# Feature-major products in two matmuls per block of 128 instead of three, and one adaLN vector computed a stage later

## The chip, the cores and the metric

The kernel runs on one core of a Trainium2 chip, as one program on five engines: TensorE (PE in the rows, with PEld for its loads of weights), VectorE (DVE), ScalarE (ACT), GpSimd (POOL) and SyncE (SP), which here only issues DMAs. The metric is the device time of one execution in microseconds (us); lower is better.

## The reference

Two transformer blocks run on 256 tokens of width 2048, all in float32. Cut to what the change touches:

```
def first_block(x, ...):
    z = rms_norm(x, pre_mix_g) @ w_in            # q, k, v, u
    ...                                           # chunked attention, multi-scale pool, w_o
    h = rms_norm(x, pre_ffn_g)
    up = causal_dwconv(h @ w_up, conv_w, conv_b)  # 3 taps over tokens
    y = (gelu(up[..., :5632]) * up[..., 5632:]) @ w_down
    return x + rms_norm(y, post_ffn_g)

def second_block(x, c, ctx, c_ctx, ...):
    shift1, scale1, gate1, shift2, scale2, gate2 = split(silu(c) @ w_ada + b_ada, 6)
    # the context gets its own shift1, scale1 from c_ctx
    hc = modulate(rms_norm(ctx, norm1_g), cshift1, cscale1)
    ...                                           # keys and values of ctx and x, attention, w_br, w_out
    h = modulate(rms_norm(x, norm2_g), shift2, scale2)
    return x + gate2 * ((silu(h @ w_ff_gate) * (h @ w_ff_up)) @ w_ff_down)
```

## The kernel before

**Products.** Each float32 operand is held as two parts, a high part h rounded to the matmul's format and the rest l, and each product is made of three matmuls, ah·bh + ah·bl + al·bh (`mm3`, L334 to L336). There are two ways to lay a product out. *Token-major* (`token_major`): 128 tokens of activations are the stationary operand, 512 columns of weights stream past them, three matmuls of 512 columns. *Feature-major* (`feature_major`): 128 columns of weights are stationary and all 256 tokens stream, so that the result has features on partitions; per block kb of 128 inputs that is three matmuls of 256 columns (weight h with activation h, weight h with activation l, weight l with activation h), and 16 blocks make one product of 48 matmuls in one PSUM bank. The kernel makes 192 feature-major products: 8 for u and 16 for q and k in block 1, 84 in the first feed-forward (42 blocks of 128 features, two halves each), 84 in the second; 192 x 16 = 3072 triplets.

**Weights.** `Stream` sends all weights in the order of use as pieces of 128x1024 through four buffers w (DMAs on SP, L203). `prep` makes their parts: ScalarE casts h (L236), VectorE subtracts l (L237), into rings of five buffers. A piece holds eight slabs of 128x128 groups; `done` is called after each slab of 512 columns, frees a buffer after every second, and emits the next `prep`.

**adaLN.** The vectors silu(c) @ w_ada + b_ada are made on VectorE: one step (L516) multiplies a 128x512 piece of w_ada with a row of silu(c) held on all partitions and sums. There are 512 steps over 384 pieces v (four buffers, DMAs on SP, L210); the first 128 pieces give shift1 and scale1 for c and for the context (two steps each), then come sh2, gate1, sc2 and gate2 with 64 pieces each. `done` emits `pace` steps per slab, by `PACE` (stage; feature-major, token-major), up to `limit` pieces; `S.finish()` emits what is left at the end of a stage.

**Side work.** Everything beside the stream of products is written as generators in `Side`; each tick (one per slab, roughly) advances at most `per` of them, and `side.drain()` ticks until all have ended, with no product emitted between. The order in which instructions are emitted is the order on each engine.

**Stages.** Block 1 (v, then q and k, then u, the other half of v, q and k, out projection), its feed-forward `ffn1` (six groups of up to eight blocks: the group's feature-major products with `act` on each, then four token-major chunks of 512 columns that add the group's part of w_down to y), then block 2: keys and values of context and x (`token_major` with four token tiles, six chunks), attention, w_br and w_out, and `ffn` again for the second feed-forward.

**The context.** During `ffn1`, `ctx_norm` normalises the context: for each of two token tiles it loads four chunks of 512 columns (L843), sums their squares, takes the factor (`rstd`, L403 to L406, the power on GpSimd), loads the chunks again (L850) and for each multiplies by the factor (L852), transposes on TensorE (L429), scales and shifts (L436 on ScalarE or L438 on VectorE, four each) and splits in h and l (L329, L330). Its loads go through two buffers. Its first act is

```
        while len(self.ada_done) < 8:
            yield 1
```

so that it starts only when the first 128 pieces of w_ada are through; it is queued at the first chunk of the third group (`gi == 2`). At the last chunk of the fifth of the six groups stands

```
            if gi == len(GROUPS) - 2 and c == 3 and t == 1:
                side.drain()
                S.finish()
                side.drain()
```

Of the kernel before, what the change touches and what calls it, by code (L numbers as in the profile page):

```python
# [33 lines left out]
PACE = ((0.6, 0.6), (0.5, 0.6), (0.0, 0.9), (0.05, 0.6), (0.2, 0.25))  # L35
# [234 lines left out]
class Kernel:  # L270
# [33 lines left out]

    def slot(self, i, dt):
        return self.spool.tile([P, 4096], dt, name=f"slot{i}", tag=f"slot{i}")
# [32 lines left out]
    def feature_major(self, xh, xl):  # L339

        bank = self.ob()
        self.S.pace = self.pace[0]
        for s in range(4):
# [232 lines left out]
    def block1(self):  # L576
# [4 lines left out]
        hh, hl = (self.slot(i, F32R).rearrange("p (k t) -> p k t", k=KB) for i in (0, 1))  # L581
# [25 lines left out]
        self.ada_begin({0: 0, 1: 4}, 192)  # L607

        ah, al = (self.slot(i, F32R).rearrange("p (k t) -> p k t", k=KB) for i in (2, 3))
# [10 lines left out]
        inv = self.g(64)  # L620
        nc.gpsimd.dma_start(tab, a["rb"])
# [35 lines left out]
        def uproj():  # L657
            for fb in range(8):
                bank = self.feature_major(hh, hl)
                nc.scalar.copy(ut[:, fb, 16:], bank[:, :256])  # L660
                if fb % 2:
                    side.add(pool(fb // 2))

        def qkproj(which):
            for j in range(4):
                bank = self.feature_major(hh, hl)
                self.split(qk[:, 2 * which, j, :], qk[:, 2 * which + 1, j, :], bank[:, :256])
# [126 lines left out]
    def out_proj(self, ah, al, state):  # L794
# [3 lines left out]
        hh, hl = (self.slot(i, F32R).rearrange("p (k t) -> p k t", k=KB) for i in (0, 1))  # L798
# [4 lines left out]
        st = {}  # L803
# [27 lines left out]
        self.ffn1(hh, hl, st["x"], lambda: self.norm_t(st["xs"], 1, hh, hl))  # L831
# [25 lines left out]
    def ffn(self, hh, hl, first, act, chunk_end, mid, tail=0):  # L857

        self.products, self.side.limit, self.side.per = 0, 5, 2
        banks = self.token_major([(hh, hl, 0), (hh, hl, 1)], self.staged(mid))  # L860
        pr = self.slot(self.prslot, F32R).rearrange("p (s k t) -> p s k t", s=2, k=8)
        first(banks, pr)
        total = 0
        for gi, grp in enumerate(GROUPS):
            last = gi == len(GROUPS) - 1
            total += len(grp)
            for n, i in enumerate(grp):
                if i > 1:
                    act(i, 0, self.feature_major(hh, hl), pr, n)
                    act(i, 1, self.feature_major(hh, hl), pr, n)  # L870
# [15 lines left out]
    def ffn1(self, hh, hl, x, mid):  # L886
        nc, a, side = self.nc, self.a, self.side
        S = self.S
# [4 lines left out]
        ch, cl = (self.slot(i, F32R).rearrange("p (k t) -> p k t", k=KB) for i in (2, 3))  # L893
# [3 lines left out]

        def act(i, half, bank, pr, n):
            f = half * NFB + i
            z = tmp[half]()  # L900
            w0, w1, w2, b = (self.vec(n, f, 1) for n in ("conv_w0", "conv_w1", "conv_w2", "conv_b"))
            nc.scalar.activation(z, bank[:, :256], AF.Identity, scale=w2, bias=b)  # L902
            nc.vector.scalar_tensor_tensor(z[:, 1:], bank[:, :255], w1, z[:, 1:], op0=ALU.mult, op1=ALU.add)  # L903
            nc.vector.scalar_tensor_tensor(z[:, 2:], bank[:, :254], w0, z[:, 2:], op0=ALU.mult, op1=ALU.add)
            if half == 0:
                za[n % 2] = z
                side.add(gelu(z))
                return

            def emit(a=za[n % 2]):  # L910
                p = pbuf()
                nc.vector.tensor_mul(p, a, z)
                return p
            side.add(self.product(pr, n, emit))

        za = {}

        def gelu(z):
            yield 1
            nc.scalar.activation(z, z, AF.Gelu_apprx_tanh)  # L920
            yield 1
# [5 lines left out]
        def chunk_end(gi, c, t, bank):  # L927
# [11 lines left out]
            if gi == len(GROUPS) - 2 and c == 3 and t == 1:  # L939
# [3 lines left out]
                assert S.vdone == 192 and len(self.ada_done) == 12  # L943
# [75 lines left out]
        h2, l2 = (self.slot(i, F32R).rearrange("p (k t) -> p k t", k=KB) for i in (0, 1))  # L1019
# [15 lines left out]
        self.ffn(hh, hl, first, act, chunk_end, mid, tail=4)  # L1035
# [31 lines left out]
    def block2(self):  # L1067
# [87 lines left out]
        oah, oal = (self.slot(i, F32R).rearrange("p (k t) -> p k t", k=16) for i in (2, 3))  # L1155
# [224 lines left out]
        mh, ml = (self.slot(i, F32R).rearrange("p (k t) -> p k t", k=KB) for i in (0, 1))  # L1380
# [34 lines left out]
        hh, hl = (self.slot(i, F32R).rearrange("p (k t) -> p k t", k=KB) for i in (2, 3))  # L1415
# [35 lines left out]
        sg, pb = self.ring(256, 2), self.ring(256, 2)  # L1451
        outr = a["out"].rearrange("(t p) d -> p t d", p=P)

        def act(i, half, bank, pr, n):
            if half == 0:
                za[n % 2] = z = sg()
                nc.scalar.activation(z, bank[:, :256], AF.Silu)
                return
            z = pb()
            nc.vector.tensor_mul(z, bank[:, :256], za[n % 2])  # L1460
            side.add(self.product(pr, n, lambda: z))

# [38 lines left out]
        self.ffn(hh, hl, first, act, chunk_end, lambda: self.norm_t(last["xs"], 1, hh, hl, self.g2, self.ada_v["sh2"]), tail=4)  # L1501
# [23 lines left out]
```

## Time and profile before

| | |
|---|---|
| time, median of three runs | 2772.29 us (2771.5 to 2775.25) |
| the profiled execution: its own time | 2772.85 us |
| its span, first to last instruction | 2771.1 us |
| PE busy | 2721.5 us, 98% of the span |
| DVE, ACT, POOL busy | 72%, 46%, 6% |
| the chain that ended last | PE 83%, DVE 3%, ACT 2% |

The span is what the trace covers; 1.75 us lie outside it. A matmul's duration in the rows is longer than the time to the next one, since matmuls overlap: how fast they follow each other is read from their starts.

### The profile page before, as it was taken

To read this page: it belongs to the slowest core of one execution; us is meant where nothing else is said; L and a number is where in the kernel's file an instruction comes from. 1 tells how busy PE (TensorE), PEld (TensorE's weight loads), DVE (VectorE), ACT (ScalarE), POOL (GpSimd) and SP (SyncE) were. 2 spreads that over 40 slices of the span, in tenths; PEclk is the share of its full clock that TensorE was granted. 3 is DMA by queue.
4 is the path that set the end of the run, shared out by engine and by line. 5 is a ranking of instruction groups with operands and counts; after the bars stand their busy time and mean duration, and the time that the engine had idled before them with its cause. 6 is when DMAs were issued, how large, how long until landed. Compare 5 with 4: busy or idle time off the path is not lost.

```text
span 2771.1 us, 43473 instructions
## 1 busy us (share of the span) xinstructions
PE 2721.5 (98%) x16726; PEld 2435.5 (88%) x16726; DVE 1986.2 (72%) x3258; ACT 1287.1 (46%) x1810; POOL 159.0 (6%) x215
## 2 busy tenths in 40 slices
PE   7999999999999999999999999999999999999999
PEld 6988798989898988788877888888889999898988
DVE  4888787888889856756477877678675565655465
ACT  4444455545455545422366665534354434343433
POOL 1010000000000000211011110100000000000000
PEclk9999999999999999999999999999999999999999
DMA  7667677676789854656555544599667676755565
GB/s 247 211 232 247 219 230 253 229 251 229 242 280 320 283 189 161 214 184 231 200 175 182 168 163 141 176 332 323 232 199 233 222 231 222 231 191 190 184 200 164
DMA packets 195696, 610.39 MB, mean 220 GB/s; under 512 B 22736, under 2 KB 22928, under 8 KB 194464
## 3 DMA queue, kind: packets, MB, share of 16 engines
q1 hardware_dynamic: 183024, 562.12, 60.5%
q0 software_dynamic: 12320, 45.25, 5.1%
q8 instruction: 131, 2.15, 0.3%
q14 instruction: 77, 0.63, 0.1%
q10 hardware_dynamic: 144, 0.25, 0.0%
HBM read 592.81 MB, written 14.71 MB: 219 GB/s over the span
## 4 chain that ended last, share of the span: by engine, by line
PE 83%; DVE 3%; ACT 2%; issue 1%; POOL 0%; ACTq 0%; DVEq 0%
PE bank L334 27%; PE bank L335 27%; PE bank L336 27%; DVE l L237 1%; PE bank L1227 1%; ACT h L236 1%; ACT G L454 0%; ACT slot L329 0%; PE bank L429 0%; ACT G L436 0%; PE bank L1201 0%; DVE slot L935 0%; PE bank L1216 0%; DVE slot L962 0%; DVE G L438 0%
## 5 line engine op out<-in xcount | busy, mean ns | idle before, releaser
L237 DVE TENSOR_TENSOR l<-w,h 128x1024 fp32r<-128x1024 f32 x870 | 1063.6, 1226 | 536.3 <-ACT h L236 526.0
L236 ACT CAST h<-w 128x1024 fp32r<-128x1024 f32 x870 | 907.8, 1049 | 842.4 <-PE bank L336 418.6
L334 PE MATMUL bank<-slot,h 128*128 128x256 f32 x3088 | 876.2, 284 | 4.4 <-DVE slot L330 4.1
L336 PE MATMUL bank<-slot,l 128*128 128x256 f32 x3088 | 875.1, 283 | 0.9 <-DVE l L237 0.9
L335 PE MATMUL bank<-slot,h 128*128 128x256 f32 x3088 | 874.9, 283 | 0.0
L334 PE MATMUL bank<-h,slot 128*128 128x512 f32 x2112 | 835.2, 395 | 9.1 <-ACT slot L329 4.3
L335 PE MATMUL bank<-l,slot 128*128 128x512 f32 x2112 | 826.7, 391 | 8.1 <-DVE l L237 8.1
L336 PE MATMUL bank<-h,slot 128*128 128x512 f32 x2112 | 826.2, 391 | 0.1
L334 PEld LDWEIGHTS bank<-slot,h 128*128 128x128 f32 x3088 | 593.9, 192 | 5.3 <-issue 4.3
L336 PEld LDWEIGHTS bank<-slot,l 128*128 128x128 f32 x3088 | 593.8, 192 | 1.2 <-DVE l L237 1.2
L335 PEld LDWEIGHTS bank<-slot,h 128*128 128x128 f32 x3088 | 593.9, 192 | 0.5
L334 PEld LDWEIGHTS bank<-h,slot 128*128 128x128 f32 x2112 | 398.4, 189 | 97.9 <-issue 7.4
L335 PEld LDWEIGHTS bank<-l,slot 128*128 128x128 f32 x2112 | 398.5, 189 | 90.2 <-DVE l L237 11.9
L336 PEld LDWEIGHTS bank<-h,slot 128*128 128x128 f32 x2112 | 398.1, 188 | 85.7 <-DVE slot L330 1.7
L516 DVE CUSTOM_DVE_ANT_0 G<-v,G 128x512 bf16<-128x512 f32 x512 | 386.7, 755 | 10.7 <-DMA v<-wada 8.5
L329 ACT CAST slot<-bank 128x512 fp32r<-128x512 f32 (+1 forms) x141 | 71.0, 528 | 131.0 <-PE bank L336 64.3
L330 DVE TENSOR_TENSOR slot<-bank,slot 128x512 fp32r<-128x512 f32 (+1 forms) x141 | 82.7, 610 | 44.4 <-ACT slot L329 44.2
L902 ACT ACTIVATE G<-bank,G 128x256 f32<-128x256 f32 x88 | 49.7, 565 | 115.5 <-PE bank L336 111.3
L903 DVE SCALAR_TENSOR_TENSOR G<-bank,G 128x255 f32<-128x255 f32 x88 | 42.4, 482 | 44.5 <-ACT G L902 44.5
L329 ACT CAST slot<-G 128x256 fp32r<-128x256 f32 (+1 forms) x114 | 52.0, 457 | 42.7 <-DVE G L438 23.9
L1244 ACT ACTIVATE G<-bank,G 128x512 f32<-128x512 f32 x64 | 49.8, 780 | 45.1 <-DVE G L1238 44.9
L330 DVE TENSOR_TENSOR slot<-G,slot 128x256 fp32r<-128x256 f32 (+1 forms) x114 | 55.3, 485 | 14.3 <-ACT slot L329 13.9
(198 smaller groups left out, 1307.6 us busy)
## 6 DMA issues: line engine op xcount, KB each, us to landing
v<-wada SPq DMA_DIRECT2D x384, 256.0 KB, 4.1
w<-wup SPq DMA_DIRECT2D x176, 512.0 KB, 4.3
w<-wgu SPq DMA_DIRECT2D x176, 512.0 KB, 3.4
w<-wdn SPq DMA_DIRECT2D x88, 512.0 KB, 4.1
w<-wfd SPq DMA_DIRECT2D x88, 512.0 KB, 3.3
w<-w SPq DMA_DIRECT2D x66, 512.0 KB, 4.6
w<-w2g SPq DMA_DIRECT2D x64, 512.0 KB, 3.3
w<-w2kv SPq DMA_DIRECT2D x52, 512.0 KB, 3.8
```

What stands on the lines that cost most here:

```text
L236: self.nc.scalar.copy(h, w)
L237: self.nc.vector.tensor_sub(l, w, h.bitcast(F32))
L329: self.nc.scalar.copy(h, src)
L330: self.nc.vector.tensor_sub(l, src, h.bitcast(F32))
L334: t.matmul(out, ah, bh, start=start, stop=False)
L335: t.matmul(out, ah, bl, start=False, stop=False)
L336: t.matmul(out, al, bh, start=False, stop=stop)
L516: nc.vector.tensor_tensor_reduce(out=self.junkv.bitcast(mybir.dt.bfloat16), in0=w, in1=self.adat[:, slot * 512:(slot + 1) * 512], scale=1. ...
L902: nc.scalar.activation(z, bank[:, :256], AF.Identity, scale=w2, bias=b)
L903: nc.vector.scalar_tensor_tensor(z[:, 1:], bank[:, :255], w1, z[:, 1:], op0=ALU.mult, op1=ALU.add)
L1227: nc.tensor.transpose(bank[:, k * P:(k + 1) * P], src[:, k * P:(k + 1) * P], self.ident)
L1244: nc.scalar.activation(d, bank, AF.Exp, bias=mx, scale=rq, accum_out=s)
```

## The change

Activations that feed feature-major products now lie in one tile of 128x8192 (`pair`) as [h of block kb, l of block kb], so that one matmul of 512 columns makes weight h with both parts; the second matmul of 256 columns adds weight l with h to the left half. The two halves of the bank are added when the bank is emptied (`folded`: a copy of the right half on ScalarE, an addition of the left half to it on VectorE), and convolution, SiLU, q and k splits then read the folded result from SBUF, mostly one product later. The vector sh2 (64 pieces of w_ada) is no longer made by the end of `ffn1` but in block 2's key and value stage, and three paces are changed.

```
-PACE = ((0.6, 0.6), (0.5, 0.6), (0.0, 0.9), (0.05, 0.6), (0.2, 0.25))
+PACE = ((0.5, 0.6), (0.27, 0.62), (0.0, 1.7), (0.05, 0.6), (0.2, 0.25))
...
+    def pair(self, i):
+        t = self.spool.tile([P, 8192], F32R, name=f"pair{i}", tag=f"pair{i}")
+        x = t.rearrange("p (k n) -> p k n", k=KB)
+        return x, x[:, :, :256], x[:, :, 256:]
...
-    def feature_major(self, xh, xl):
+    def feature_major(self, x):
...
-                self.mm3(bank[:, :256], h[:, j * P:(j + 1) * P], l[:, j * P:(j + 1) * P],
-                         xh[:, kb, :], xl[:, kb, :], kb == 0, kb == KB - 1)
+                hj, lj = h[:, j * P:(j + 1) * P], l[:, j * P:(j + 1) * P]
+                if kb < KB - 1:
+                    t.matmul(bank, hj, x[:, kb, :], start=kb == 0, stop=False)
+                    t.matmul(bank[:, :256], lj, x[:, kb, :256], start=False, stop=False)
+                else:
+                    t.matmul(bank[:, :256], lj, x[:, kb, :256], start=False, stop=False)
+                    t.matmul(bank, hj, x[:, kb, :], start=False, stop=True)
...
+    def folded(self, bank, out):
+        z = self.half()
+        self.nc.scalar.copy(z, bank[:, 256:])
+        self.nc.vector.tensor_add(out, bank[:, :256], z)
+        return out
...
-        if kind == 0:
-            self.ada_begin({k: k for k in range(4)}, self.S.limit)
...
-        self.ada_begin({0: 0, 1: 4}, 192)
+        self.ada_begin({0: 0, 1: 4}, 128)
...
-                bank = self.feature_major(hh, hl)
-                nc.scalar.copy(ut[:, fb, 16:], bank[:, :256])
+                self.folded(self.feature_major(hx), ut[:, fb, 16:])
...
         def act(i, half, bank, pr, n):
+            last = i == NFB - 1 or i % 8 == 7
+            if i > 1:
+                side.until(lambda: half not in busy)
+                busy.add(half)
+                bank = self.folded(bank, xq[half])
+            gen = acted(i, half, bank[:, :256], pr, n, int(i > 1 and not last))
+            if last or i < 2:
+                next(gen)
+            side.add(gen)
...
-                assert S.vdone == 192 and len(self.ada_done) == 12
+                assert S.vdone == 128 and len(self.ada_done) == 8
```

**TensorE, a feature-major product of `ffn1`.** The tile numbers after the names are buffers; bank is PSUM, slot and pair hold the activations, h and l the parts of the weights; the last column is the output. Before:

```order
L334 MATMUL bank_71<-slot_2138,h_82 128x256
L335 MATMUL bank_71<-slot_2139,h_82 128x256
L336 MATMUL bank_71<-slot_2138,l_87 128x256
L334 MATMUL bank_71<-slot_2138,h_82 128x256
L335 MATMUL bank_71<-slot_2139,h_82 128x256
L336 MATMUL bank_71<-slot_2138,l_87 128x256
```

and of the change:

```order
L358 MATMUL bank_73<-pair_1775,h_85 128x512
L359 MATMUL bank_73<-pair_1775,l_90 128x256
L358 MATMUL bank_73<-pair_1775,h_85 128x512
L359 MATMUL bank_73<-pair_1775,l_90 128x256
```

Two instructions stand for three, and the columns are the same, 768 per block.

**TensorE, the context's transposes.** Before, the transposes of a context chunk (L429) stand alone among products; this is the second of the eight:

```order
L429 MATMUL bank_74<-G 128x128 x4
L334 MATMUL bank_72<-slot_2138,h_86 128x256
L335 MATMUL bank_72<-slot_2139,h_86 128x256
L336 MATMUL bank_72<-slot_2138,l_91 128x256
```

In the change (L450 is the same line) the first of the eight stands among the products of the fifth group's third and fourth chunk; the other seven stand in one piece, at the fifth group's last chunk (L342 to L344 are its token-major matmuls), ahead of the first feature-major product of the sixth group:

```order
L342 MATMUL bank_72<-h_84,slot_2671 128x512
L343 MATMUL bank_72<-l_89,slot_2671 128x512
L344 MATMUL bank_72<-h_84,slot_2671 128x512
L450 MATMUL bank_74<-G 128x128 x4
L450 MATMUL bank_75<-G 128x128 x4
L450 MATMUL bank_76<-G 128x128 x4
L450 MATMUL bank_77<-G 128x128 x4
L450 MATMUL bank_74<-G 128x128 x4
L450 MATMUL bank_75<-G 128x128 x4
L450 MATMUL bank_76<-G 128x128 x4
L358 MATMUL bank_73<-pair_1775,h_85 128x512
```

**VectorE at the same place of the change.** L981 adds the last chunk to y, L879 multiplies a context chunk by its factor, L459 scales and shifts four blocks, L338 is the low part of a split, L424 and L426 are `rstd`, L238 is the low part of a piece of weights.

```order
L981 TENSOR_TENSOR slot_2515<-bank_72,slot_2515 128x512
L338 TENSOR_TENSOR pair_2516<-G,pair_2516 128x4x128
L879 TENSOR_SCALAR G<-G 128x512
L459 TENSOR_SCALAR G<-bank_75,G 128x128 x4
L338 TENSOR_TENSOR pair_2516<-G,pair_2516 128x4x128
L879 TENSOR_SCALAR G<-G 128x512
L338 TENSOR_TENSOR pair_2516<-G,pair_2516 128x4x128
L424 TENSOR_REDUCE G<-G 128x1
L426 TENSOR_SCALAR G<-G 128x1
...
L879 TENSOR_SCALAR G<-G 128x512
L338 TENSOR_TENSOR pair_2516<-G,pair_2516 128x4x128
L238 TENSOR_TENSOR l_89<-w_80,h_84 128x1024
```

Before, VectorE has pieces of weights, `act` and adaLN steps between one context chunk's operations and the next one's; here it has none of them between the last addition to y and the next piece of weights.

## Rows read from the trace of the kernel before

**Rows 1.** The page: busy time, share of the span and instructions of the engines.
```profile
PE 2721.5 (98%) x16726; PEld 2435.5 (88%) x16726; DVE 1986.2 (72%) x3258; ACT 1287.1 (46%) x1810; POOL 159.0 (6%) x215
```

**Rows 2.** The page, costliest groups: line, engine, operation, output<-inputs, sizes, count | busy us, mean ns | idle just before and who ended most of it. The first two are one of the three feature-major lines and one of the three token-major lines.
```profile
L334 PE MATMUL bank<-slot,h 128*128 128x256 f32 x3088 | 876.2, 284 | 4.4 <-DVE slot L330 4.1
L334 PE MATMUL bank<-h,slot 128*128 128x512 f32 x2112 | 835.2, 395 | 9.1 <-ACT slot L329 4.3
L516 DVE CUSTOM_DVE_ANT_0 G<-v,G 128x512 bf16<-128x512 f32 x512 | 386.7, 755 | 10.7 <-DMA v<-wada 8.5
```

**Rows 3.** Timeline of TensorE, start us, duration us, where a feature-major product of `ffn1` ends and a token-major chunk begins. Between the first row shown and the second lie 32 matmuls of 256 columns, between the last two lie 31 of 512.
```profile
699.74 0.28 PE L336 MATMUL bank<-slot,l 128*128 128x256 f32 x1
...
703.70 0.28 PE L336 MATMUL bank<-slot,l 128*128 128x256 f32 x1
703.82 0.40 PE L334 MATMUL bank<-h,slot 128*128 128x512 f32 x1
704.05 0.40 PE L335 MATMUL bank<-l,slot 128*128 128x512 f32 x1
...
704.52 0.40 PE L334 MATMUL bank<-h,slot 128*128 128x512 f32 x1
...
711.78 0.39 PE L336 MATMUL bank<-h,slot 128*128 128x512 f32 x1
```

**Rows 4.** Busy time by stretches: from:to, length, then busy us of each engine (instructions), granted clock of PE, share of DMA, GB/s. In turn: u in block 1; a stretch of `ffn1` with feature-major products alone; the fifth group's feature-major part, with context work; one chunk of keys in block 2's key and value stage.
```profile
112.00:157.00 45.00, 42.24 (x320) 40.40 (x319) 40.08 (x79) 20.33 (x39) 12.24 (x8) 0.96 0.55 175
500.00:550.00 50.00, 50.00 (x419) 50.00 (x418) 44.05 (x79) 25.86 (x35) 0.00 (x0) 1.00 0.65 225
890.00:925.00 35.00, 35.00 (x295) 35.00 (x295) 33.39 (x64) 19.36 (x30) 0.54 (x1) 1.00 0.85 290
1234.00:1278.00 44.00, 43.90 (x194) 36.05 (x193) 30.62 (x59) 10.81 (x13) 8.99 (x9) 1.00 0.59 207
```

**Rows 5.** Groups by line and shape, columns as in rows 2: operations of 256 columns that read a PSUM bank.
```profile
L660 ACT COPY G<-bank 128x256 f32<-128x256 f32 x8 | 3.0, 380 | 0.0
L902 ACT ACTIVATE G<-bank,G 128x256 f32<-128x256 f32 x88 | 49.7, 565 | 115.5 <-PE bank L336 111.3 <-DVE G L904 2.6 <-PE bank L1030 1.6
L1460 DVE TENSOR_TENSOR G<-bank,G 128x256 f32<-128x256 f32 x42 | 17.9, 425 | 24.4 <-PE bank L336 24.3
```

**Rows 6.** Timelines of single engines, context work in `ffn1`: start, duration, engine, line. The two GpSimd rows are the power in `rstd` and the second loads; then VectorE's multiplication of a chunk by the factor and its part of `rstd`, and the sum of a chunk's squares on ScalarE.
```profile
789.05 1.52 POOL L406 TENSOR_TENSOR G<-G 128x1 f32<-128x1 f32 x1 [10.38 <-DVE G L405]
790.54 1.11 POOL L850 DMA_DIRECT2D G<-ctx  x2
811.46 0.48 DVE L852 TENSOR_SCALAR G<-G 128x512 f32<-128x512 f32 x1
788.63 0.15 DVE L403 TENSOR_REDUCE G<-G 128x1 f32<-128x4 f32 x1
788.81 0.15 DVE L405 TENSOR_SCALAR G<-G 128x1 f32<-128x1 f32 x1
777.13 0.63 ACT L454 ACTIVATE G<-G 128x512 f32<-128x512 f32 x1
777.66 0.19 ACT L454 ACTIVATION_READ_ACCUMULATOR G<-G 128x1 f32 x1
```

**Rows 7.** The chain that ended last, start, duration, what: the same kinds of operations one behind the other (a chunk's multiplication, its four scalings, cast and subtraction), where x is normalised after `ffn1`.
```profile
1112.99 0.72 ACT G L973
1114.26 1.42 ACT G L436 x4
1115.70 0.63 ACT slot L329
1116.35 0.69 DVE slot L330
```

**Rows 8.** Time from issue to landing of the context's loads (256 KB each), first and second ones; then of w_ada's pieces, and of the key and value spills, in the key and value stage.
```profile
DMA to landing us min/median/max: 3.3/5.4/7.4
DMA to landing us min/median/max: 3.6/6.2/7.5
v<-wada SPq DMA_DIRECT2D x64, 256.0 KB, 3.7
kv<-slot POOLq DMA_DIRECT2D x24, 256.0 KB, 3.0
```

**Rows 9.** Timeline of TensorE: the transposes of the context's last chunk, between two matmuls of 256 columns.
```profile
897.13 0.28 PE L336 MATMUL bank<-slot,l 128*128 128x256 f32 x1
897.25 0.60 PE L429 MATMUL bank<-G 128*128 128x128 f32 x4
897.60 0.36 PE L334 MATMUL bank<-slot,h 128*128 128x256 f32 x1
897.80 0.28 PE L335 MATMUL bank<-slot,h 128*128 128x256 f32 x1
```

**Rows 10.** Busy time by stretches, as rows 4, around the norm ahead of `ffn1`, where TensorE waits for VectorE and ScalarE.
```profile
330.00:335.00 5.00, 2.43 (x10) 1.23 (x8) 4.30 (x8) 1.67 (x5) 0.55 (x1) 1.00 0.28 105
335.00:340.00 5.00, 3.51 (x10) 2.32 (x11) 4.86 (x7) 4.40 (x10) 0.00 (x0) 0.66 0.44 125
340.00:345.00 5.00, 5.00 (x24) 4.03 (x23) 4.30 (x9) 1.00 (x3) 0.55 (x1) 0.66 0.58 189
345.00:350.00 5.00, 5.00 (x26) 4.13 (x24) 5.00 (x7) 4.49 (x7) 0.00 (x0) 1.00 0.13 45
```

**Rows 11.** Timeline at the end of `ffn1`'s last feature-major product: the last matmul of 256 columns is followed by the first of 512; then VectorE's last product of the two halves and its low part.
```profile
1068.37 0.40 PE L334 MATMUL bank<-h,slot 128*128 128x512 f32 x1
1069.17 0.48 DVE L903 SCALAR_TENSOR_TENSOR G<-bank,G 128x255 f32<-128x255 f32 x1 [1.30 <-ACT G L902]
1071.25 0.42 DVE L912 TENSOR_TENSOR G<-G 128x256 f32<-128x256 f32 x1
1072.14 0.43 DVE L330 TENSOR_TENSOR slot<-G,slot 128x256 fp32r<-128x256 f32 x1 [0.47 <-ACT slot L329]
```

More of the change, by code (lines that the diff above doesn't have):

```diff
@@ L620, in block1, with half @@
         inv = self.g(64)
+        xq = [self.xs_[:, i * 256:(i + 1) * 256] for i in range(4)]
+        zk = [0]
+        def half():
+            zk[0] += 1
+            return xq[2 + zk[0] % 2]
+        self.half = half
         nc.gpsimd.dma_start(tab, a["rb"])
@@ L664, in qkproj @@
         def qkproj(which):
-            for j in range(4):
-                bank = self.feature_major(hh, hl)
-                self.split(qk[:, 2 * which, j, :], qk[:, 2 * which + 1, j, :], bank[:, :256])
+            z = None
+            for j in range(5):
+                last, z = z, self.folded(self.feature_major(hx), xq[j % 2]) if j < 4 else None
+                if j:
+                    self.split(qk[:, 2 * which, j - 1, :], qk[:, 2 * which + 1, j - 1, :], last)
         def mix():
@@ L797, in out_proj @@
         self.rows = self.ring(512, 2)
-        hh, hl = (self.slot(i, F32R).rearrange("p (k t) -> p k t", k=KB) for i in (0, 1))
+        hx, hh, hl = self.pair(0)
         ss = [self.ss[:, :4], self.ss[:, 4:]]
@@ L884, in product, with ffn1 @@
         yield 1
-    def ffn1(self, hh, hl, x, mid):
+    def ffn1(self, pair, x, mid):
         nc, a, side = self.nc, self.a, self.side
@@ L892, in ffn1 @@
         self.prslot = 6
-        ch, cl = (self.slot(i, F32R).rearrange("p (k t) -> p k t", k=KB) for i in (2, 3))
+        _, ch, cl = self.pair(2)
         tmp = [self.ring(256, 2) for _ in range(2)]
@@ L896, in ffn1, with half_, conv @@
         ss = [self.ss[:, :4], self.ss[:, 4:]]
-        def act(i, half, bank, pr, n):
-            f = half * NFB + i
+        xq = [self.xs_[:, k * 256:(k + 1) * 256] for k in range(4)]
+        zk, busy, za, gelus = [0], set(), {}, set()
+        def half_():
+            zk[0] += 1
+            return xq[2 + zk[0] % 2]
+        self.half = half_
+        def conv(f, z, src):
+            w0, w1, w2, b = (self.vec(n, f, 1) for n in ("conv_w0", "conv_w1", "conv_w2", "conv_b"))
+            nc.scalar.activation(z, src, AF.Identity, scale=w2, bias=b)
+            nc.vector.scalar_tensor_tensor(z[:, 1:], src[:, :255], w1, z[:, 1:], op0=ALU.mult, op1=ALU.add)
+            nc.vector.scalar_tensor_tensor(z[:, 2:], src[:, :254], w0, z[:, 2:], op0=ALU.mult, op1=ALU.add)
@@ new lines, in act, with acted @@
+        def act(i, half, bank, pr, n):
+            last = i == NFB - 1 or i % 8 == 7
[7 more added lines that the diff above has]
+            side.add(gen)
+        def acted(i, half, src, pr, n, wait):
+            if wait:
+                yield wait
@@ L900, in act @@
             z = tmp[half]()
[L901 to L904, printed above, removed]
+            conv(half * NFB + i, z, src)
+            busy.discard(half)
@@ L905, in act @@
+            yield 1
             if half == 0:
-                za[n % 2] = z
-                side.add(gelu(z))
+                nc.scalar.activation(z, z, AF.Gelu_apprx_tanh)
+                za[i] = z
                 return
[L910 to L921, printed above, removed]
+            yield from self.product(pr, n, lambda: product(i, z), 0)
@@ L1018, in ffn1 @@
         self.normed = set()
[L1019 removed]
+        _, h2, l2 = self.pair(0)
         self.x2 = self.dpool.tile([P, 2, D], F32, name="x2")
@@ L1414, in block2 @@
         ss = [self.ss[:, :4], self.ss[:, 4:]]
-        hh, hl = (self.slot(i, F32R).rearrange("p (k t) -> p k t", k=KB) for i in (2, 3))
+        hx, hh, hl = self.pair(2)
         y = self.slot(4, F32)
@@ L1499, in first @@
             self.products += 2
-        self.ffn(hh, hl, first, act, chunk_end, lambda: self.norm_t(last["xs"], 1, hh, hl, self.g2, self.ada_v["sh2"]), tail=4)
+        self.ffn((hx, hh, hl), first, act, chunk_end, lambda: self.norm_t(last["xs"], 1, hh, hl, self.g2, self.ada_v["sh2"]), tail=4)
         side.drain()
```

38 lines of the change are left out of this document (25 added, 13 removed).

## The prediction

> **What bounds the kernel now.** The page comes first: TensorE is busy for 98% of the span, VectorE for 72% [rows 1]. A busy share says nothing about pace, so the timeline is next: in the feed-forward, matmuls of 256 columns start every (703.82 - 699.74) / 34 = 0.1200 us and those of 512 every (711.78 - 704.52) / 32 = 0.2269 us, without a gap where one kind follows the other [rows 3]. The extra 256 columns cost 0.1069 us, so each matmul carries some 0.013 us that do not depend on its columns. Third, the stretches: where feature-major products stand alone, TensorE is never idle while VectorE is busy for 44 of 50 us [rows 4]. TensorE's stream of matmuls is the bound there, and VectorE is near enough to it to be watched.
>
> **The change, part by part.** *The pair.* A block cost 3 x 0.1200 = 0.3600 us and will cost 0.2269 + 0.1200 = 0.3469 us: the columns stay 768, one fixed part of 0.0131 us goes. Over 3072 blocks that is **-40.2 us**. The trace has no stretch in which the two sizes alternate; where one kind gives way to the other the starts are 0.12 and 0.23 apart, each by the size of the earlier matmul [rows 3], so I add. Bounds: nothing saved (0.3600), or the second matmul without a fixed part of its own (0.3338, -80 us).
>
> The Trainium skill ("TensorE: Matmul & The Clock Gate", Back-to-back issue gap) gives a matmul N / 2.4 ns and only 2.5 ns on top at full clock. By that rule the dropped matmuls would be worth 3072 x 2.5 ns = 7.7 us and the sum would be 32 us higher. Here it speaks against the change; the rows have 13 ns instead.
>
> *The folds.* 192 copies on ScalarE and 192 additions on VectorE, at 0.38 and 0.42 us by the nearest rows (0.565 is the dearest) [rows 5]. In `ffn1` a product took VectorE 44.05 / 50 x 5.76 = 5.07 us [rows 4]; the addition brings 0.42, the pace of 0.27 for 0.5 takes away 4 x 0.23 x 0.755 = 0.69 [rows 2]: 4.80 us of a product's new 5.55 us, 86% against 88%. Work in hand (up to five buffers of weights, each worth two slabs) covers them: nothing. In the second feed-forward VectorE has more room still. While u is made, VectorE is busy for 40.1 of 45 us and TensorE has lost 2.8 already [rows 4]. There eight additions bring 3.4 us, the lower pace takes 2.4, and TensorE's part shrinks by 1.7: 41.1 of 43.3 us, 95%. That cover is thin, and the stage behind it starts with fewer buffers in hand: **+2 us** (0 to 5).
>
> *The end of `ffn1`.* Before, the last low part was ready at 1072.57 [rows 11]; the last of four blocks of the following chunk needs it 18 matmuls of 0.2269 = 4.08 us after 1068.37, at 1072.45. The fold puts 0.38 + 0.42 in front: **+0.8 us**. The five earlier groups have 42 matmuls, 9.5 us, of cover: nothing.
>
> *sh2 later.* 64 steps and 64 loads move to the key and value stage. In a chunk of keys VectorE had 30.6 of 44 us [rows 4]; 0.8 x 16 = 12.8 more steps of 0.755 bring 9.7: 92%. Loads: 1.7 pieces per slab of 12 x 0.2269 = 2.72 us are needed, 0.62 per us; four buffers that each take 3.7 us to land [rows 8] and 0.755 to use allow 0.90. Both fit, but the emptying of banks at a chunk's end stands behind one or two more steps, and the next chunk's fourth tile needs such a bank: **+1 us** (0 to 4). SP's loads of weights stand behind more waits for v, but have four buffers.
>
> *The context.* Nothing in the diff names it, and it is what decides. `ctx_norm` waits for shift1 and scale1, that is for adaLN step 256. With paces of 0.5 and 0.27 that step now comes near the end of the fifth group, where `side.drain()` stands. So seven of eight chunks are normalised with no product between: the seven groups of transposes stand in one piece on TensorE, and VectorE's order there is one chain. Before, all of it was spread among products that hid it. I walk the chain from the fifth group's last matmul. A chunk takes 0.48 (multiplication) [rows 6], and from the end of such a multiplication at 1113.71 to the end of the subtraction at 1117.04 it is 3.33 us (transposes, four scalings, cast, subtraction) [rows 7]: 3.8 in all. Chunk 1's multiplication is already done: 3.5, with handovers. Chunks 2 and 3: 11.1. Of the second tile's squares the first chunk's load has landed by then; the second's buffer is free only now. A load takes 3.3 us at the shortest and 5.4 and 6.2 in the middle [rows 8], all while the queues were full; in the burst SP stands still, so 3.5 is an estimate near the short end. Load 3.5 and squares 0.75 give 15.35; the fourth load and its squares 19.6; `rstd` 0.3 + 1.5 [rows 6], 21.4; the first chunk again, 24.9; three chunks, 36.3; the last multiplication and transposes 0.9: TensorE is back at its products after **37.2 us**. The seven groups of transposes cost 0.43 each among products (897.13 to 897.80, less one matmul of 0.12 and less 0.12 for the first one behind them) [rows 9], 3.0 in all, which go. Net **+34.2 us**. Bounds: 32.7 with loads of 3.0, the shortest row [rows 8]; 45 with loads of 5.8, which come on top five times (chunk 3, the second and fourth squares, the first reload and the third).
>
> *The clock.* After such gaps the granted clock fell to the lower of its two levels, 1.2 instead of 2.4 GHz: behind a stretch with TensorE half idle two slices of 5 us show 0.66, and then 1.00 again [rows 10]. Lost there: 2 x 5 x 0.34 = 3.4 us. Part may fall into the wait: **+3 us** (0 to 3.4).
>
> **Sum.** -40.2 + 34.2 + 3 + 2 + 1 + 0.8 = +0.8 us on the profiled execution's 2772.85 (a span of 2771.1 and 1.75 around it): 2773.65. That execution is 0.56 above the median of the runs, so the forecast for the median is **2773 us**: the gain on TensorE is real, and one burst eats it.
>
> **The rivals.**
> 1. *Faster: the alternating pair is cheaper than its parts.* Place: the 3072 pairs. Against it: in both uniform streams every matmul has its 13 ns [rows 3]. For it: no row shows alternation, and behind a 512-column matmul the next load of weights has twice the time. From a pair of 0.3449 us on (2 ns less) the result counts as faster; at its bound of 0.3338 it would be 2733.
> 2. *Slower: the burst's loads land as under load*, 5.8 us: +11, 2784. For it: two pieces of weights are still on their way when it begins. Against it: afterwards nothing else is.
> 3. *Slower: w_ada's loads bound the key and value stage.* If they took 6.5 us to land, a step would take 7.25 / 4 = 1.81 us, 128 of them 232 us in place of 204: +27, 2800. Against it: 3.7 us before [rows 8].
> 4. *The change doesn't do what it says: the fixed part stays, and a pair costs the 0.3600 us of three*: +40.2, 2813. Against it: the 13 ns of every matmul in rows 3. The Trainium skill's 2.5 ns (the section named above) are a milder form of it, with which the time would be some 2805.
>
> **How the numbers follow.** A difference of 0.2%, 5.5 us, is about what a measurement of this kernel can tell from none; "same" is 2766.7 to 2777.8. The forecast has 0.55, its own range being 2765 to 2780 (the bounds of the small terms and of the clock): 0.06 of it faster, 0.43 same, 0.06 slower. Rival 1 has 0.21, rival 2 0.14, rival 3 0.04, rival 4 0.06. So faster 0.27, same 0.43, slower 0.30. The range takes in rival 2 and the near half of rival 1: 2760 to 2788 us.
>
> **What would show it.** Right: in feature-major stretches starts 0.227 and 0.120 us apart, alternating; the sixth group's first feature-major product 35 to 40 us behind the fifth group's last chunk, with seven groups of transposes between, TensorE waiting for VectorE at each, and a granted clock below 1 just behind; `ffn1`'s feature-major part otherwise without a wait. Wrong: a pair well off 0.347; a burst under 30 us; waits of TensorE for weights' low parts all through `ffn1` or the key and value stage.

## The result and the profile after

The change made the kernel slower: **2805.86 us** (2804.66 to 2808.34) against 2773.31 us of the kernel before, a ratio of 1.0118 [1.0101, 1.0136]. The forecast of 2773 us and its range of 2760 to 2788 us both missed; "slower" had 0.30. The profiled execution of the changed kernel took 2804.66 us, its span is 2802.9 us, 31.8 us longer than the span before. Of all executions reported here one, the tenth of experiment 7, ran at a granted clock of 0.849 and took 2969.84 us, and the ratios leave it out.

The page of the changed kernel, the busy shares and four of the costliest groups (columns as in [rows 1] and [rows 2]); L358 and L359 are the two matmuls of a block, L371 the addition of the fold, L537 the adaLN step:

```profile
PE 2711.1 (97%) x13654; PEld 2275.9 (81%) x13654; DVE 2059.3 (73%) x3450; ACT 1343.5 (48%) x1994; POOL 151.0 (5%) x211
...
L358 PE MATMUL bank<-pair,h 128*128 128x512 f32 x2880 | 1029.2, 400 | 4.3 <-DVE slot L338 4.0
L359 PE MATMUL bank<-pair,l 128*128 128x256 f32 x2880 | 810.4, 281 | 0.9 <-DVE l L238 0.9
...
L537 DVE CUSTOM_DVE_ANT_0 G<-v,G 128x512 bf16<-128x512 f32 x512 | 383.8, 750 | 37.3 <-DMA v<-wada 33.8
...
L371 DVE TENSOR_TENSOR G<-bank,G 128x256 f32<-128x256 f32 x192 | 81.4, 424 | 91.5 <-ACT G L370 90.9
```

TensorE has 3072 matmuls less and its busy time falls by only 10 us, while its idle time grows from 49.6 to 91.8 us. Steps now wait for their piece of w_ada for 33.8 us, against 8.5 [rows 2]. The pace is again read from starts. TensorE's timeline in a feature-major product of `ffn1` (start us, duration us):

```profile
501.39 0.40 PE L358 MATMUL bank<-pair,h 128*128 128x512 f32 x1
501.63 0.28 PE L359 MATMUL bank<-pair,l 128*128 128x256 f32 x1
501.74 0.40 PE L358 MATMUL bank<-pair,h 128*128 128x512 f32 x1
501.99 0.28 PE L359 MATMUL bank<-pair,l 128*128 128x256 f32 x1
502.11 0.40 PE L358 MATMUL bank<-pair,h 128*128 128x512 f32 x1
502.34 0.28 PE L359 MATMUL bank<-pair,l 128*128 128x256 f32 x1
502.45 0.40 PE L358 MATMUL bank<-pair,h 128*128 128x512 f32 x1
```

Three pairs take 502.45 - 501.39 = 1.06 us, 0.3533 each, not 0.3469. Over some 150 undisturbed products the starts give 5653 ns a product, 0.3533 us a pair: 236.2 ns from a 512 to the 256 behind it, 117.1 from that to the next 512.

Stretches of the changed kernel (columns as in [rows 4]): u in block 1; a stretch of `ffn1` with products alone; the burst and the 10 us behind it; 50 us of the key and value stage.

```profile
112.00:157.00 45.00, 39.37 (x212) 33.18 (x212) 36.96 (x78) 20.10 (x39) 8.12 (x6) 0.92 0.49 163
500.00:550.00 50.00, 50.00 (x285) 43.39 (x284) 41.76 (x73) 27.64 (x43) 0.00 (x0) 1.00 0.66 210
...
1015.00:1055.00 40.00, 6.51 (x25) 4.60 (x26) 11.26 (x27) 10.85 (x26) 7.49 (x14) 0.53 0.30 94
1055.00:1060.00 5.00, 5.00 (x22) 4.29 (x22) 1.92 (x2) 3.84 (x7) 0.00 (x0) 0.69 0.09 36
1060.00:1065.00 5.00, 5.00 (x30) 4.37 (x30) 3.17 (x4) 2.10 (x4) 0.00 (x0) 1.00 0.66 203
...
1293.00:1318.00 25.00, 22.37 (x99) 18.21 (x97) 19.10 (x42) 6.50 (x8) 1.81 (x2) 0.99 0.92 309
1318.00:1343.00 25.00, 24.28 (x96) 19.85 (x96) 22.03 (x44) 4.22 (x4) 7.07 (x7) 0.87 0.62 203
```

The burst on TensorE, from the fifth group's last matmul through the seven groups of transposes (L450) to the sixth group's first pair; in brackets the idle time ahead and its releaser:

```profile
1013.96 0.39 PE L344 MATMUL bank<-h,slot 128*128 128x512 f32 x1
1014.19 0.60 PE L450 MATMUL bank<-G 128*128 128x128 f32 x4
1018.16 1.11 PE L450 MATMUL bank<-G 128*128 128x128 f32 x4 [3.38 <-DVE G L879]
1022.61 1.09 PE L450 MATMUL bank<-G 128*128 128x128 f32 x4 [3.33 <-DVE G L879]
1040.67 1.12 PE L450 MATMUL bank<-G 128*128 128x128 f32 x4 [16.97 <-DVE G L879]
...
1054.02 1.09 PE L450 MATMUL bank<-G 128*128 128x128 f32 x4 [3.33 <-DVE G L879]
1054.76 0.78 PE L358 MATMUL bank<-pair,h 128*128 128x512 f32 x1
```

and VectorE in it (L879 multiplies a chunk by its factor, L424 begins `rstd`):

```profile
1017.63 0.48 DVE L879 TENSOR_SCALAR G<-G 128x512 f32<-128x512 f32 x1
...
1021.98 0.48 DVE L879 TENSOR_SCALAR G<-G 128x512 f32<-128x512 f32 x1
...
1035.44 0.16 DVE L424 TENSOR_REDUCE G<-G 128x1 f32<-128x4 f32 x1 [8.77 <-ACT G L475]
...
1040.12 0.49 DVE L879 TENSOR_SCALAR G<-G 128x512 f32<-128x512 f32 x1 [4.34 <-DMA G<-ctx]
...
1044.48 0.48 DVE L879 TENSOR_SCALAR G<-G 128x512 f32<-128x512 f32 x1
```

The burst is where it was forecast: 1054.76 - 1014.19 = 40.6 us without a product, 37.2 forecast. A chunk takes 4.35 us (1017.63 to 1021.98), not 3.8: the granted clock is 0.53 of full speed, so four transposes last 1.1 us instead of the 0.60 of [rows 9].

**Where the 31.8 us lie.** The n-th token-major matmul is the same work in both programs, so the difference of its starts, after less before, shows what was won and lost up to it (the alignment, below). Feature-major products between two such places are taken at their own gain of 107 ns each.

| place | forecast, us | measured, us |
|---|---|---|
| 3072 pairs | -40.2 | 3072 x (0.3533 - 0.3600) = -20.6 |
| the burst, and the clock behind it | +37.2 and +3 | +42.1 |
| block 1 (q, k, u) | +2 | +3.7 |
| `ffn1`'s first five groups otherwise (the transposes that leave them) | -3.0 | -1.6 |
| end of `ffn1`, and up to the key and value stage | +0.8 | +1.3 and +1.0 |
| key and value stage | +1 | +5.8 |
| start and everything else | 0 | +0.1 |
| sum | +0.8 | +31.8 |

Block 1's term is that of one execution: with the start counted in it is 4.0 us here, and in the traces of experiments 6, 7 and 9, which have the same paces there, 4.4, 7.0 and 3.6.

### The profile page after: what moved, and what is told of

Read it like the earlier page. It is cut to its first block, busy times and chain, and to the rows that moved or that the text cites. A ratio compares the mean times of both kernels' runs of the same rounds, so it can differ in the third digit from the quotient of the medians.

```text
span 2802.9 us, 37671 instructions
## 1 busy us (share of the span) xinstructions
PE 2711.1 (97%) x13654; PEld 2275.9 (81%) x13654; DVE 2059.3 (73%) x3450; ACT 1343.5 (48%) x1994; POOL 151.0 (5%) x211
## 4 chain that ended last, share of the span: by engine, by line
PE 79%; DVE 4%; ACT 2%; issue 1%; DMA 1%; POOL 0%; ACTq 0%; DVEq 0%; POOLq 0%
PE bank L358 21%; PE bank L342 15%; PE bank L344 15%; PE bank L343 15%; PE bank L359 11%; PE bank L362 1%; DVE l L238 1%; PE bank L361 1%; PE bank L1273 1%; DMA v<-wada 1%; ACT h L237 1%; DVE G L537 1%; PE bank L450 0%; ACT G L475 0%; ACT pair L337 0%
## 5 line engine op out<-in xcount | busy, mean ns | idle before, releaser
L238 DVE TENSOR_TENSOR l<-w,h 128x1024 fp32r<-128x1024 f32 x870 | 1061.8, 1224 | 412.6 <-ACT h L237 400.5
L358 PE MATMUL bank<-pair,h 128*128 128x512 f32 x2880 | 1029.2, 400 | 4.3 <-DVE slot L338 4.0
L359 PE MATMUL bank<-pair,l 128*128 128x256 f32 x2880 | 810.4, 281 | 0.9 <-DVE l L238 0.9
L358 PEld LDWEIGHTS bank<-pair,h 128*128 128x128 f32 x2880 | 542.9, 189 | 129.6 <-issue 4.3
L359 PEld LDWEIGHTS bank<-pair,l 128*128 128x128 f32 x2880 | 545.4, 189 | 10.2 <-DVE l L238 1.4
L342 PE MATMUL bank<-h,pair 128*128 128x512 f32 x1344 | 538.4, 401 | 15.4 <-ACT h L237 7.2
L343 PE MATMUL bank<-l,pair 128*128 128x512 f32 x1344 | 529.8, 394 | 8.8 <-DVE l L238 8.7
L344 PE MATMUL bank<-h,pair 128*128 128x512 f32 x1344 | 529.4, 394 | 0.1
L537 DVE CUSTOM_DVE_ANT_0 G<-v,G 128x512 bf16<-128x512 f32 x512 | 383.8, 750 | 37.3 <-DMA v<-wada 33.8
L342 PEld LDWEIGHTS bank<-h,pair 128*128 128x128 f32 x1344 | 255.3, 190 | 75.0 <-ACT h L237 10.1
L342 PE MATMUL bank<-h,slot 128*128 128x512 f32 x768 | 299.2, 390 | 2.2 <-ACT slot L337 2.2
L344 PEld LDWEIGHTS bank<-h,pair 128*128 128x128 f32 x1344 | 255.2, 190 | 56.5 <-DVE pair L338 2.3
L343 PE MATMUL bank<-l,slot 128*128 128x512 f32 x768 | 298.8, 389 | 0.0
L344 PE MATMUL bank<-h,slot 128*128 128x512 f32 x768 | 298.8, 389 | 0.0
L342 PEld LDWEIGHTS bank<-h,slot 128*128 128x128 f32 x768 | 144.2, 188 | 32.2 <-ACT slot L337 3.1
L344 PEld LDWEIGHTS bank<-h,slot 128*128 128x128 f32 x768 | 144.2, 188 | 30.4 <-DVE slot L338 0.3
L371 DVE TENSOR_TENSOR G<-bank,G 128x256 f32<-128x256 f32 x192 | 81.4, 424 | 91.5 <-ACT G L370 90.9
L362 PE MATMUL bank<-pair,h 128*128 128x512 f32 x192 | 76.7, 400 | 0.0
```

Source lines behind the costliest of these rows:

```text
L238: self.nc.vector.tensor_sub(l, w, h.bitcast(F32))
L342: t.matmul(out, ah, bh, start=start, stop=False)
L343: t.matmul(out, ah, bl, start=False, stop=False)
L344: t.matmul(out, al, bh, start=False, stop=stop)
L358: t.matmul(bank, hj, x[:, kb, :], start=kb == 0, stop=False)
L359: t.matmul(bank[:, :256], lj, x[:, kb, :256], start=False, stop=False)
```

## The experiments

Ratios are against the kernel before, run on the same chip.

**1. The new products with the old adaLN schedule.**

```
-PACE = ((0.5, 0.6), (0.27, 0.62), (0.0, 1.7), (0.05, 0.6), (0.2, 0.25))
+PACE = ((0.6, 0.6), (0.5, 0.6), (0.0, 0.9), (0.05, 0.6), (0.2, 0.25))
...
+        if kind == 0:
+            self.ada_begin({k: k for k in range(4)}, self.S.limit)
...
-        self.ada_begin({0: 0, 1: 4}, 128)
+        self.ada_begin({0: 0, 1: 4}, 192)
...
```

> The pair and the folds alone: limits, paces and the place of sh2 as in the kernel before. Theory (the account of the two traces: the pair takes 0.3533 us in place of 0.3469, so it saves 20.6 us and not 40.2; the burst of the context costs 39; the key and value stage 6; block 1 some 4.6): no burst and no longer key and value stage, so 2772.9 - 20.6 + 2 to 6 for block 1 and the ends of groups = 2754 to 2760 us. Rival 1 (the folds make VectorE the bound of the first feed-forward: 5.07 + 0.42 = 5.49 of 5.65 us per product, 97%): waits of TensorE for low parts of weights all through it, 2770 us or more. Rival 2 (the pair is slow only where VectorE or the loads are late, and would take 0.3469 otherwise): 2733 to 2740 us.

Measured: 2790.38 us, 1.006 [1.0045, 1.0075]. No burst and no loss in the key and value stage, but still slower than before, and 30 us above the top of the theory. The waits of TensorE in the first feed-forward, us in total, times, longest; L342 and L344 stand at the ends of four groups, L450 are transposes of the context:

```profile
PE bank L342 <- ACT slot L337: 10.4, 4, 2.9
PE bank L450 <- DVE G L881: 4.2, 2, 2.9
PE bank L344 <- DVE slot L338: 3.9, 4, 1.0
```

By the alignment of the table above, the four ends cost 22.9 us: these 14.3 us of waits, and for most of the rest the granted clock behind them (0.66 from 450 to 455 us, 0.67 from 590 to 595 and from 730 to 735). Another 6.4 us go in the products ahead of the fourth end, where the context's transposes wait.

The first group's end shows how they come about: TensorE's first token-major matmul there and the two that wait, then VectorE's last low part.

```profile
435.37 0.40 PE L342 MATMUL bank<-h,slot 128*128 128x512 f32 x1
...
447.92 0.50 PE L342 MATMUL bank<-h,slot 128*128 128x512 f32 x1 [2.86 <-ACT slot L337]
449.62 0.50 PE L344 MATMUL bank<-h,slot 128*128 128x512 f32 x1 [0.97 <-DVE slot L338]
```

```profile
442.51 0.42 DVE L371 TENSOR_TENSOR G<-bank,G 128x256 f32<-128x256 f32 x1
447.01 0.42 DVE L968 TENSOR_TENSOR G<-G 128x256 f32<-128x256 f32 x1
449.15 0.42 DVE L338 TENSOR_TENSOR slot<-G,slot 128x256 fp32r<-128x256 f32 x1
```

The last fold starts 442.51 - 435.37 = 7.1 us into the chunk, since VectorE still has earlier work to do, and the low part is done at 449.57, 14.2 us in, where 42 matmuls cover 9.5. In the changed kernel the same three rows are

```profile
432.79 0.40 PE L342 MATMUL bank<-h,slot 128*128 128x512 f32 x1
```

```profile
435.71 0.42 DVE L371 TENSOR_TENSOR G<-bank,G 128x256 f32<-128x256 f32 x1
439.56 0.42 DVE L966 TENSOR_TENSOR G<-G 128x256 f32<-128x256 f32 x1
441.70 0.43 DVE L338 TENSOR_TENSOR slot<-G,slot 128x256 fp32r<-128x256 f32 x1
```

with the low part done 9.3 us in, just inside the cover. So the first rival was right that VectorE is late at the old pace, though it had the waits spread over the products: most of them stand at the ends of groups. Whether it is the folds or the shorter products that make it late was not separated. The new pace of 0.27 buys that cover, and the same pace brings the burst.

**2. The changed kernel with step 256 early.**

```
-PACE = ((0.5, 0.6), (0.27, 0.62), (0.0, 1.7), (0.05, 0.6), (0.2, 0.25))
+PACE = ((0.6, 0.6), (0.5, 0.6), (0.0, 1.7), (0.05, 0.6), (0.2, 0.25))
```

> The change with the paces of before in block 1 and the first feed-forward, so that adaLN step 256 comes as early as before and the context starts in the third group; sh2 stays in the key and value stage. Theory (the burst costs 39 us): 2805.9 - 39 = 2767 us, 2763 to 2771, with waits of TensorE of 3 to 6 us left in the key and value stage. Rival (the burst hides behind something else, or what it costs comes back as VectorE load in the feed-forward): above 2785 us.

Measured: 2783.77 us, 1.0034 [1.0021, 1.0047], above the theory's range and 1 us under the rival's bound. The burst is gone, but three group ends wait as in the first experiment (7.8 us for the high part, 1.9 for the low), and the key and value stage keeps its 5.7 us. The rival's second half, that the cost comes back in the feed-forward, is largely what happened.

**3. The kernel before with the context queued two groups later.**

```
-            if gi == 2 and c == t == 0:
+            if gi == 4 and c == t == 0:
```

> The kernel before with one edit: the context is queued at the fifth group's first chunk in place of the third's, so that it drains in one piece as in the change. Theory: the burst alone, +39 us on 2772.9: 2808 to 2815 us, TensorE idle for some 40 us ahead of the sixth group. Rival (the burst costs only together with the pair or the later adaLN): under 2785 us.

Measured: 2816.67 us, 1.0154 [1.0139, 1.0169]: +43 us from one moved queueing, with products, paces and sh2 as before. TensorE's waits there, on the line that multiplies a context chunk:

```profile
PE bank L429 <- DVE G L852: 37.0, 7, 17.1
```

A late context alone costs about what it cost in the changed kernel (42.1 - 1.6 = 40.5 us net of the transposes that leave the products), without pairs or folds.

**4. Runs of four matmuls of one size.** Per slab four matmuls of 512 columns, then four of 256 (the last slab the other way round).

```
...
+                def hs(js=js, last=last):
+                    for j in js:
+                        kb = 4 * s + j
+                        t.matmul(bank, h[:, j * P:(j + 1) * P], x[:, kb, :], start=kb == 0, stop=last and kb == KB - 1)
...
+                for part in (ls, hs) if last else (hs, ls):
+                    part()
...
```

> The change with another order inside a product: for each slab the four matmuls of 512 columns, then the four of 256. Theory A (it is the alternation of sizes that costs 6.4 ns a pair; in uniform runs each matmul takes 0.2269 and 0.1200): one change in four pairs, 3072 x 3/4 x 6.4 ns = 15 us less, 2791 us. Theory B (the extra belongs to the 512-column matmul with activations moving, whatever stands beside it): unchanged, 2803 to 2809 us, starts 0.236 apart inside the runs.

Measured: 2797.22 us, 1.0085 [1.0068, 1.0102], between the two: 5600 ns a product, neither the 5547 of the sum nor the 5653 of alternation.

**5. Runs of eight,** 512, 256, 256, 512, two slabs held at a time.

```
...
+        for s0 in range(0, 4, 2):
+            w = [self.S.get(i) for i in range(2)]
...
+            for part in (ls, hs) if s0 // 2 % 2 else (hs, ls):
+                part()
...
```

> The changed kernel with the sixteen blocks of a product in four runs of eight matmuls of one size: 512, 256, 256, 512 columns (the next product begins with 512 again). Two slabs of weights are held at a time. Theory (a step from 256 columns to 512 is what costs, alternation is its many repeats): a product has one such step and not sixteen; with the 9 ns by which a 512 behind a 256 exceeds one behind a 512, and four or five matmuls after a change at half that, it takes 5547 + 15 to 25 = 5562 to 5572 ns, -81 to -91 ns for each of 192 products: 2788 to 2791 us. Rival (any product that mixes the two sizes into one bank pays, in whatever order): 5653 ns as in the changed kernel, or about 5600 as with runs of four: 2796 to 2806 us.

Measured: 2792.72 us, 1.0067 [1.005, 1.0084]; 5567 ns a product, as the theory had it. The time is 2 us above its range; by the alignment, block 1 took 3.4 us more than in the changed kernel at the same paces. TensorE's timeline, where equal matmuls stand in one row (start of the first, x count):

```profile
501.22 2.08 PE L364 MATMUL bank<-pair,l 128*128 128x256 f32 x16
503.13 3.82 PE L359 MATMUL bank<-pair,h 128*128 128x512 f32 x16
506.79 2.08 PE L364 MATMUL bank<-pair,l 128*128 128x256 f32 x16
508.70 3.59 PE L359 MATMUL bank<-pair,h 128*128 128x512 f32 x15
```

Sixteen of 256 take 1.91 us, 0.1194 each; sixteen of 512 take 3.66, 0.2288 each. By position, as means over some 140 products: the first five 512s behind a run of 256s take 233, 236, 228, 233 and 231 ns, all later ones 226.7; the first two 256s behind 512s take 113 and 119, all later ones 120.0. One change from 256 to 512 and back costs 27.3 - 7.5 = 20 ns. Runs of four have three such changes, (5600 - 5547) / 3 = 18 ns each; alternation has fifteen, 7 ns each.

The kernel before has the same steps where its products meet its chunks: at eleven undisturbed places the first five 512s behind 256s take 233, 236, 228, 232 and 231 ns in the median, and the first two 256s behind 512s 113 and 119. There the 512s have weights moving and not activations. What the places have in common is the change of size.

**6. The low part added into the other half of the bank.**

```
...
-                    t.matmul(bank[:, :256], lj, x[:, kb, :256], start=False, stop=False)
+                    t.matmul(bank[:, 256:], lj, x[:, kb, :256], start=False, stop=False)
```

> The changed kernel with the low part's matmul of 256 columns added into the right half of the bank instead of the left; the sum of both halves is the same. Theory (the size of the matmul before is what counts): a pair stays at 0.353 us, 2804 to 2808 us. Rival (the 512 that follows waits for the columns that the 256 has just added into, which come first in the bank): pairs fall towards 0.347 us, 3072 x 0.006 = -18 us, about 2787 us.

Measured: 2806.46 us, 1.0118 [1.0103, 1.0133], 5653 ns a product: no difference. Which half of the bank the 256 columns go to does not matter.

**7. A pace in between.**

```
-PACE = ((0.5, 0.6), (0.27, 0.62), (0.0, 1.7), (0.05, 0.6), (0.2, 0.25))
+PACE = ((0.5, 0.6), (0.36, 0.72), (0.0, 1.7), (0.05, 0.6), (0.2, 0.25))
```

> The changed kernel with the pace of adaLN steps in the first feed-forward at 0.36 and 0.72 instead of 0.27 and 0.62. In the order of instructions the context's transposes then stand spread among products, and VectorE gets 0.09 x 4 x 0.755 = 0.27 us more per product, 5.07 of 5.65 us or 90%. Theory (the burst of 41 us is the whole of what the late step 256 costs, and the waits at group ends of the schedule of before came from VectorE at 97%): the burst goes, the group ends stay covered, 2765 to 2773 us. Rival (any pace at which the context comes early takes the cover from the group ends): waits of 4 to 6 us at three or four group ends return, 2780 to 2790 us.

Measured: 2769.66 us, 0.9983 [0.9973, 0.9992], 36 us below the changed kernel. The burst is gone, as the theory had it; the group ends are not quite covered and wait 4.2 us in all. The first one, TensorE and VectorE:

```profile
435.36 0.40 PE L342 MATMUL bank<-h,slot 128*128 128x512 f32 x1
...
446.99 0.50 PE L344 MATMUL bank<-h,slot 128*128 128x512 f32 x1 [1.49 <-DVE slot L338]
```

```profile
446.52 0.41 DVE L338 TENSOR_TENSOR slot<-G,slot 128x256 fp32r<-128x256 f32 x1
```

The low part is done 11.6 us in, between the 9.3 and 14.2 of the paces on either side. The "97%" in the expectation does not hold as a mean: from 500 to 550 us VectorE is busy for 43.74 us at the old pace, 43.01 here and 41.76 in the changed kernel, 87, 86 and 84%. What differs is how late it is when the group ends.

**8. Runs of eight with that pace.** The edits of 5 and 7 together.

> Runs of eight matmuls and the paces 0.36 and 0.72 together. Theory: both gains add, -41 and -16 us from the changed kernel's 2806, less what VectorE lacks as products get shorter (5.07 of 5.56 us, 91%): 2745 to 2758 us, faster than the kernel before by 15 to 28 us. Rival: products shorter by 0.09 us take the cover away, waits at group ends of 10 to 20 us in all, 2765 to 2775 us.

Measured: 2756.42 us, **0.994 [0.9925, 0.9954]**, faster than both kernels: 17 us less than before, 49 less than the change. Both gains add (13 us from experiment 5, 36 from experiment 7); 5567 ns a product, and the group ends wait 5.8 us instead of 4.2.

**9. sh2 left out.**

```
-PACE = ((0.5, 0.6), (0.27, 0.62), (0.0, 1.7), (0.05, 0.6), (0.2, 0.25))
+PACE = ((0.5, 0.6), (0.36, 0.72), (0.0, 0.9), (0.05, 0.6), (0.2, 0.25))
...
-        S.vitems = self.ada_items([("sh1", "csh1"), ("sc1", "csc1")], 0) + self.ada_items(["sh2"], 3) \
-            + self.ada_items(["gate"], 2) + self.ada_items(["sc2"], 4) + self.ada_items(["gate"], 5)
+        S.vitems = self.ada_items([("sh1", "csh1"), ("sc1", "csc1")], 0) + self.ada_items(["gate"], 2) + self.ada_items(["sc2"], 4) + self.ada_items(["gate"], 5)
...
```

> The kernel with paces 0.36 and 0.72, without the vector sh2: its 64 adaLN steps and their 64 loads are left out (the vector is zero), and the key and value stage has the pace of 0.9 again. Theory (the step that appeared in that stage, 5 us against the kernel before, is the price of sh2's steps: a step that waits for its load stands ahead of the emptying of a bank): TensorE loses nothing there, as in the kernel before, and the time falls by 4.5 to 6 us from 2769.7: 2764 to 2765 us. Rival (the stage loses its 5 us to something else that the change brought there): 2769 to 2770 us.

Measured: 2765.0 us, 0.9972 [0.9962, 0.9982], 4.7 us below experiment 7 by the medians, 3 by the two ratios. VectorE's waits for pieces of w_ada in the key and value stage, first the changed kernel (experiment 7 has 28.4 us in 28 waits), then this one:

```profile
DVE G L537 <- DMA v<-wada: 25.1, 26, 3.3
```

```profile
DVE G L537 <- DMA v<-wada: 1.4, 3, 0.5
```

and by the alignment TensorE loses nothing there, where experiment 7 lost 4.8 us and the changed kernel 5.8. These are the price of sh2's steps and loads.

**10. Fewer steps ahead of the bank that was late.**

```
...
+                self.pace = (0.0, 1.2 if c == 3 else 1.8)
```

> Runs of eight with paces 0.36 and 0.72, and in the key and value stage 1.2 steps per slab in the chunk at whose end TensorE waited 2.9 us for a bank, 1.8 in the other four. Nothing is left out: 4 x 16 x 1.8 + 16 x 1.2 = 134 steps are room for 128. Theory (the wait is that of single steps with their loads, ahead of the bank's emptying on VectorE): the wait goes with its trail of half clock, 2756.4 - 4 to 5.5 = 2751 to 2752 us. Rival (the loads are the bound, at 306 to 319 GB/s in half of that stage: what is taken from one chunk is missing in the others): the wait comes at another chunk's end, 2755 to 2760 us.

Measured: 2754.33 us, 0.9935 [0.992, 0.995]; its profiled execution, 2759.55 us, is the longest of its four, so the time can't be told from experiment 8's. The trace tells more: the wait for the bank is gone, and another has taken its place at the end of the stage, where the transpose of gate1 waits for the last step.

```profile
PE bank L564 <- DVE G L542: 5.5, 1, 5.5
```

By the alignment the stage costs 6.9 us here and 5.6 in experiment 8, so nothing was gained. That fits the rival: from 1340 us on VectorE waits 6.2 us for pieces of w_ada, and a wait taken from one place comes up at another. It is one trace, of the longest execution.

## Why the prediction was wrong

**The pair: the sum was wrong, by 20 us.** The step that failed is "each by the size of the earlier matmul [rows 3], so I add". This term alone, -20.6 for -40.2, takes the forecast to 2793 us and out of its range; of the 31.0 us by which the sum was off, sh2 is another 4.8 and all other terms 6.6. The one change of size in [rows 3] did show the excess: from 703.82 to 704.52 three matmuls of 512 take 0.70 us, 0.2333 each, where the 32 from there on take 0.2269. I read 0.23 at the seam as the size and took the long-run pace from the rows behind it. Rival 1 had the opposite sign, and rival 4 (no gain) is half true: the saving is 6.7 ns a block, not 13.1. Experiments 4 and 5 show that order sets it, 5653, 5600 and 5567 ns for runs of one, four and eight; 6 excludes the half of the bank. What in TensorE makes a 512 behind a 256 longer was not found.

The 2.5 ns of the Trainium skill ("TensorE: Matmul & The Clock Gate", Back-to-back issue gap), which that section gives for an isolated matmul and not for a stream with loads of weights, would have given 2805 us. The time came out there, but not by that rule: long runs in experiment 5 still have 120.0 and 226.7 ns, 13.3 above N / 2.4, and the dropped matmuls gave 20.6 us, not 7.7. That the numbers agree is luck: the pairs' 19.6 us and 11.4 us of other misses add up to nearly the 32 by which that rule raises the sum.

**The burst: right in place, chain and cause, 2 us short.** 37.2 us and 3 for the clock were forecast, 40.6 and 1.6 (5 us at 0.69) measured. The clock falls inside the burst and not only behind it, which lengthens each chunk: six of the seven groups of transposes take some 0.5 us more than at full clock, which is most of the 3.4 us. The nine loads of the context from 1010 to 1056 (KB each, median us to landing) land as assumed, 3.5, and rival 2 (5.8) fell:

```profile
G<-ctx POOLq DMA_DIRECT2D x9, 256.0 KB, 3.3
```

**The folds: "nothing" was true by little.** At the fourth group's end TensorE waited 1.2 us for a high part; at the first group's end the last low part took 9.3 us of a cover of 9.5 in the changed kernel, 11.6 and 14.2 at faster paces. My reason, a busy share of 86% and five buffers in hand, was not what decides: it is how late VectorE is when a group ends, and so how much work stands around the group's last fold. Block 1 cost 3.7 in that execution against +2 (0 to 5).

**sh2: +1 forecast, +5.8 measured,** above its bound of 4. The mechanism was named (emptying of banks behind a step), but I took the landing of 3.7 us as fixed and forgot that a step that waits for its load holds up everything behind it: 25.1 us of such waits on VectorE, one bank late by 3.3 us (TensorE's only wait of the stage, below), and a granted clock of 0.87 from 1318 to 1343 us, behind it.

```profile
PE bank L342 <- DVE slot L1188: 3.3, 1, 3.3
```

Rival 3, loads as the bound, is partly right: w_ada's pieces landed in 4.1 us in the middle and not in its 6.5, but from 1293 to 1318 DMA moves 309 GB/s at a share of 0.92, against 207 GB/s at 0.59 in a chunk of keys before [rows 4]. The Trainium skill ("DMA: Bandwidth & Descriptors", Specifications) puts a core's limit at some 358 GB/s; 309 is 86% of it. Single slices of 5 us of this stage show up to 383, so this trace does not bear it out as a ceiling, and no row shows what held the 25 us at 309.

In the forecast the pairs' gain and the burst cancelled. With half the gain, and sh2 at almost six times its price, most of the burst is left over.

## What to carry to other kernels

When a seam between two kinds of instruction is the whole of a change's inner loop, take the pace from the rows at the seam, not from the runs on either side, and where the seam costs, lengthen the runs. Ask of a slack engine not its busy share but how late its last operation is when the stage ends, against the cover in microseconds. A pace that cures lateness delays whatever waits for the last step; look for the pace at which neither binds, and count a wait for a load as time of everything queued behind it.

## What the runs showed of the hardware

A matmul of 512 columns behind one of 256 starts the next one 236 ns later instead of 226.7, and after a run of 256s the first five are long (233, 236, 228, 233, 231 ns); one of 256 behind 512s takes 113 instead of 120.0. In alternation this repeats in a period of three pairs, 1.06 us. It does not depend on which half of the bank is written (5653 ns a product either way). And 40 us without products cost only 1.6 us behind them (5 us at a clock of 0.69), but more inside, where 24 transposes of 28 ran at half clock.
